# A decoder layer on one core: weight sums ordered behind a plain block, and three PSUM bank assignments changed

## The chip, the core and the metric

The kernel runs on one core of a Trainium2 chip. The metric is the device time of one execution in microseconds (us), and the time of a kernel is the median of several executions. The profile beside it was taken of one further execution.

## What is computed

The reference is one layer over 512 tokens of 1024 features, all in float32: a half-step gated feed-forward block (FFN), a token mixer, and a second half-step FFN. In the mixer half of the width runs a gated linear recurrence and the other half attention with eight heads, both from one input projection.

```python
x = x + 0.5 * swiglu(rms_norm(x, ffn1_norm), w_gate, w_up, w_down)   # 1024 -> 2816 -> 1024
h = rms_norm(x, mix_norm)
xr, gate, q, k, v = split(h @ w_in)              # five parts of 512 features
y_rnn = rg_lru(conv4(xr)) * gelu(gate)
y_att = stick_breaking(rms_norm(q), rms_norm(k), v)   # 8 heads of 64
x = x + concat(rms_norm(y_rnn), rms_norm(y_att)) @ w_out
x = x + 0.5 * swiglu(rms_norm(x, ffn2_norm), ...)
```

## The kernel before

Activations lie transposed, features on the 128 partitions and the 512 tokens along the row, so `x` is eight tiles of 128x512. For accuracy every float32 operand is split into a rounded high part and the remainder (names with `h` and `l`: `h_ga` and `l_ga` for a gate weight, `xh` and `xl` for an activation, `hha` and `hla` for a hidden block), and a product is three matmuls, high by high, low by high, high by low (`mm3`). ScalarE (ACT) makes the high parts and VectorE (DVE) the low ones. Names end in `a` for the first FFN and `b` for the second.

**An FFN** has 22 blocks of 128 hidden features, each with a gate product `pg` and an up product `pu`. The first six are *plain* (three pairs of two): `products` runs 24 matmuls of 128x512 each for `pg` and `pu`, and `plain` then multiplies both by the norm factor `rb` into `gg` and `uu` (L267, L269), applies Silu to `gg` (L268), multiplies the two (L270) and splits the result (L254, L255). The other sixteen are computed in pairs by a seven-product scheme (`fast`). It needs sums of the activations (`bs`, split into `xh_s` and `xl_s`, made by `operands`), and, for every pair and each of gate and up, four sums of quarters of the weights: `matrix` loads the pair's weights into `raw` (tiles `rg`, `ru`) and VectorE makes the sums into `sums` (tiles `sg`, `su`) by the four additions L326, L328, L329 and L330. The second overwrites a quarter that the first has read, so the other three follow the first. Down-projections `pd` follow after blocks 6, 12, 18 and 22, eight products each, and VectorE adds them to `x` (L433).

**The mixer** projects the eight normed tiles `xh_m`, `xl_m` by `project(j)` (for j from 0 to 3: two products `pxr` and `pga`, alternating over the eight tiles for j = 0) and by `project_qkv` (for q, k and v four token blocks each, `pq`, `pk`, `pv`, the weights arriving in four parts `kk`). `norm_heads` makes normed tiles `natq` and `natk` from `pq` and `pk`: ScalarE squares, VectorE sums (`m8`, L688 and L689), GpSimd (POOL) takes the power (`r8`, L691), VectorE multiplies (`nat`, L694). `turn` transposes each `nat` on TensorE into `ptq` or `ptk` (L710). Behind the v products `rnn_out` prepares the recurrence's output (`yrh`, `yrl`, L644 and L646), and the first products with `w_out` (weights `h_o`, `l_o`) follow.

**PSUM.** `psum` opens a pool of the eight banks for a stage and `bank(name, tag)` takes one. FFN: four banks tagged `b` and four `y`; mixer: six `b` and two `y`. A bank that is taken again waits for the last reader of what lay in it, also across stages. In a stage of the mixer `y` holds the norm's two small products (`pst_m`, `psr_m`), the gates `pa`, `px`, and the turned k.

**Order.** A scheduler of the language sets each engine's order when the kernel is built, by its own estimate of times; engines then run strictly in that order and wait on semaphores. `tc.issue_after(ins)` puts what is traced inside it behind `ins` on the same engine. `tc.high_priority` raises a load and its split. All loads stand on SyncE's one queue (SP), which issues them in order as weight buffers come free.

Of the kernel before, what the change touches and what calls it, by code (L numbers as in the profile page):

```python
# [23 lines left out]
NB = T // P  # L24
# [4 lines left out]
PLAIN = 6  # L29
# [19 lines left out]
def hybrid_layer_kernel(  # L49
# [17 lines left out]
    nc = tc.nc  # L67
# [18 lines left out]
    def f32(ap):  # L86
        return ap.bitcast(F32)

    def bank(name, tag="b"):
        return banks["pool"].tile([P, T], F32, tag=tag, name=name, bufs=banks["tags"][tag])  # L90
# [40 lines left out]
    def weights_early(*args):  # L131
        with tc.high_priority(offset=200):
            return weights(*args)
# [80 lines left out]
    def ffn(name, xn, wg, wu, wd, first, done):  # L214
        def products(f, between=None):
            n = f"{name}{f}"
            c = f % 2 * KD * P
            gh, gl = weights(wg[f // 2][:, c : c + KD * P], f"g{n}")
            uh, ul = weights(wu[f // 2][:, c : c + KD * P], f"u{n}")
            pg, pu = (bank(f"{p}{n}", "y" if between else "b") for p in ("pg", "pu"))  # L220
            each = ((pg, gh, gl), (pu, uh, ul))
            order = [(e, k) for e in each for k in range(KD)]
            if f == 0:
                order = [(e, k) for k in range(KD) for e in each]
            for i, ((pt, wh, wl), k) in enumerate(order):
                s = slice(k * P, (k + 1) * P)
                mm3(pt, wh[:, s], wl[:, s], xn.h[k], xn.l[k], k == 0, k == KD - 1)
                if between and i == KD - 1:
                    between()
            return pg, pu  # L230
# [5 lines left out]
        with tc.tile_pool(name=f"ffn_{name}", bufs=1, reuse_waits="tile") as fp:  # L236

            def flat(ap):
                return ap.rearrange("p c t -> p (c t)")

            def pair_tiles(p):
                n = f"{name}{p}"
                g = fp.tile([P, 4, TH], F32, tag="g", name=f"gg{n}", bufs=2)
                u = fp.tile([P, 4, TH], F32, tag="u", name=f"uu{n}")
                return g, u
# [12 lines left out]
            def plain(p, i):  # L258

                g, u = pair_tiles(p)  # L260
                for t in range(2):
                    f = 2 * p + t
                    if f == len(ahead):
                        ahead.append(products(f))
                    gg, uu = flat(g[:, 2 * t : 2 * t + 2, :]), flat(u[:, 2 * t : 2 * t + 2, :])
                    pg, pu = ahead[f]
                    nc.vector.tensor_mul(gg, pg, rb)  # L267
                    nc.scalar.activation(gg, gg, AF.Silu)  # L268
                    nc.vector.tensor_mul(uu, pu, rb)  # L269
                    nc.vector.tensor_mul(uu, uu, gg)  # L270
                return split(u, p, i)


# [44 lines left out]

            def matrix(w, c, p):

                n = f"{c}{name}{p}"
                q = 4 * P
                raw = fp.tile([P, 4, q], F32, tag="raw", name=f"r{n}", bufs=3)
                nc.sync.dma_start(raw, w[p].rearrange("p (s w) -> p s w", s=4))
                sums = fp.tile([P, 3, q], F32, tag="sums", name=f"s{n}", bufs=2)
                nc.vector.tensor_add(sums[:, 1, :], raw[:, 2, :], raw[:, 0, :])  # L326
                s1 = raw[:, 0, :]
                nc.vector.tensor_add(s1, s1, raw[:, 1, :])  # L328
                nc.vector.tensor_add(sums[:, 0, :], raw[:, 2, :], s1)  # L329
                nc.vector.tensor_add(sums[:, 2, :], raw[:, 3, :], sums[:, 0, :])  # L330
                groups = [
                    [raw[:, 2:4, :]],
                    [sums[:, 0:1, :], raw[:, 0:1, :]],
                    [sums[:, 1:3, :]],
                    [raw[:, 1:2, :]],
                ]
                ws = []

                def get(group):
                    if group < len(ws):  # L340
                        return ws[group]
                    width = sum(a.shape[1] for a in groups[group]) * q
                    hi = wpool.tile([P, width], F32R, tag="wh", name=f"h_{n}{group}", bufs=4)
                    lo = wpool.tile([P, width], F32R, tag="wl", name=f"l_{n}{group}", bufs=4)
                    o = 0
                    for a in groups[group]:
                        a = flat(a)
                        to = slice(o, o + a.shape[1])
                        nc.scalar.copy(hi[:, to], a)
                        nc.vector.tensor_sub(lo[:, to], a, f32(hi[:, to]))  # L350
                        o += a.shape[1]
                    ws.append((hi, lo))
                    return hi, lo

                px, py = (bank(f"p{i}{n}", "b")[:, :TH] for i in "xy")

                def product(pt, group, half, b, start):
                    wh, wl = get(group)
                    for k in range(KD // 2):
                        s = slice((half * 4 + k) * P, (half * 4 + k + 1) * P)  # L360
                        bh, bl = held[k, b]
                        for i, (l, r) in enumerate(((wh, bh), (wh, bl), (wl, bh))):
                            nc.tensor.matmul(  # L363
                                pt, l[:, s], r, start=start and k == 0 and i == 0,
                                stop=k == KD // 2 - 1 and i == 2, skip_group_check=True,
                            )

                return [
                    (px, 0, 0, B11, True), (py, 0, 1, B21, True),
                    (px, 1, 0, T2, False), (py, 1, 1, T1, True),  # L370
                    (px, 2, 0, T3, False), (py, 2, 1, B22, False),
                    (px, 3, 0, T4, False),
                ], product
# [39 lines left out]
            for nf in CHUNKS:  # L413
                hs = []
                for i in range(nf // 2):
                    p = f0 // 2 + i
                    hs += (plain if 2 * p < PLAIN else fast)(p, i)
                last = f0 + nf == NF
                for k in range(KD):
                    n = f"{name}{f0}_{k}"  # L420
# [6 lines left out]
                    for t0, t1 in zip(cuts, cuts[1:]):  # L427
                        t = slice(t0, t1)
                        pt = bank(f"pd{n}_{t0}", "y")
# [17 lines left out]
    pt = bank("warm")  # L447
# [110 lines left out]
    def project(j, between=None):  # L558

        ws = [weights_early(w_rg[c], f"{n}{j}") for c, n in ((j, "xr"), (NJ + j, "ga"))]  # L560
        pts = [bank(f"p{n}{j}") for n in ("xr", "ga")]
        order = [(i, k) for i in range(2) for k in range(KD)]
        if j == 0:
            order = [(i, k) for k in range(KD) for i in range(2)]
        for i, k in order:
            s = slice(k * P, (k + 1) * P)
            (wh, wl), ks = ws[i], [kk for ii, kk in order if ii == i]
            mm3(pts[i], wh[:, s], wl[:, s], nm.h[k], nm.l[k], k == ks[0], k == ks[-1])
            if between and (i, k) == order[KD - 1]:
                between()  # L570
        return pts
# [86 lines left out]
    v = []  # L658

    def project_qkv(c, n, between):  # L660
        pts = [bank(f"p{n}{b}") for b in range(NB)]
        done = 0
        for kk in range(KD // 2):
            wh, wl = weights_early(w_qkv[c, kk], f"{n}{kk}")
            ks = (2 * kk, 2 * kk + 1)
            order = [(k, b) for k in ks for b in range(NB)]
            if kk == KD // 2 - 1 or n == "v" and kk == 0:
                order = [(k, b) for b in range(NB) for k in ks]
            for k, b in order:
                t = slice(b * P, (b + 1) * P)  # L670
                s = slice((k % 2) * DR, (k % 2 + 1) * DR)
                mm3(pts[b], nm.h[k][:, t], nm.l[k][:, t], wh[:, s], wl[:, s], k == 0, k == KD - 1)
                done += 1
                if done in between:
                    between[done]()
        return pts
# [27 lines left out]

    def turn(n, nats):
        for b, nat in enumerate(nats):
            pt = bank(f"pt{n}{b}", "b" if n == "q" else "y")
            for j in range(NJ):
                s = slice(j * P, (j + 1) * P)
                nc.tensor.transpose(pt[:, s], nat[:, s], ident)  # L710
            gain = gq if n == "q" else gk
            dh = qkT[n + "h"][:, :, b * P : (b + 1) * P]
            dl = qkT[n + "l"][:, :, b * P : (b + 1) * P]
            src = pt.rearrange("p (j t) -> p j t", j=NJ)
            nc.scalar.activation(dh, src, AF.Copy, scale=gain)
            nc.vector.scalar_tensor_tensor(
                dl, src, gain, f32(dh), op0=ALU.mult, op1=ALU.subtract
            )
# [288 lines left out]
```

## Time and profile before

| | |
|---|---|
| time, three executions | 934.52, 935.11, 940.92 us; median 935.11 us |
| the profiled execution, its own time | 937.35 us |
| its span, from first to last instruction | 935.6 us |
| its mean granted TensorE clock | 0.995 of full speed |
| TensorE busy | 916.2 us of the span |
| VectorE, ScalarE, GpSimd busy | 677.0, 443.3, 109.6 us |
| DMA | 89.51 MB, mean 96 GB/s |

A row of the timeline gives the start, the duration, the engine, the source line, the operation with its output and inputs, and in square brackets how long the engine had been idle and what ended that. A row of the waits gives the waiting and the releasing operation, the total in us, how often, and the longest. A row of the windows gives a stretch, its length, then for each engine the busy time and the number of instructions, then the granted TensorE clock (1.00 is full speed), the DMA share and GB/s. Matmuls overlap: a 128x512 one lasts 0.39 us in the rows and starts every 0.23 us.

### The profile page before, as it was taken

The numbers are of one execution on the slowest core, as the hardware profiler recorded it, in microseconds if no ns is written. First come the engines' busy times: TensorE is split into PE (matmuls) and PEld (weight loads), VectorE is DVE, ScalarE is ACT, GpSimd is POOL, SyncE is SP. The second block draws the span as 40 slices with busy tenths as digits, with TensorE's granted clock in tenths as the row PEclk, the third lists the DMA queues.
The fourth block names the chain that finished last, engine by engine and source line by source line (L and its number), as shares of the span: only waits on it lengthen the run. The fifth ranks groups of instructions, "written<-read, shape, count | busy, mean of one in ns | idle before, by whom it ended". The sixth has DMA issues, their size and how long they took to land.

```text
span 935.6 us, 13626 instructions
## 1 busy us (share of the span) xinstructions
PE 916.2 (98%) x5410; PEld 800.3 (86%) x5410; DVE 677.0 (72%) x1007; ACT 443.3 (47%) x739; POOL 109.6 (12%) x79
## 2 busy tenths in 40 slices
PE   8899999999999998999989999999999999999998
PEld 6788899889988997888866667888899989998997
DVE  7699588648864859756669867778768846884673
ACT  7154355425542546345656744454345524552451
POOL 4000000000000005554351121400000000000000
PEclk9999999999999999999999999999999999999999
DMA  7621222522252123222110112532222422243102
GB/s 248 241 75 51 68 91 91 162 64 91 91 168 74 47 90 112 91 91 90 46 56 35 47 67 87 204 104 68 85 90 91 141 85 91 91 143 100 46 24 90
DMA packets 26943, 89.51 MB, mean 96 GB/s; under 512 B 2944, under 2 KB 5248, under 8 KB 22784
## 3 DMA queue, kind: packets, MB, share of 16 engines
q1 hardware_dynamic: 26880, 88.65, 28.1%
q8 instruction: 42, 0.69, 0.3%
q14 instruction: 21, 0.17, 0.1%
HBM read 86.54 MB, written 2.10 MB: 95 GB/s over the span
## 4 chain that ended last, share of the span: by engine, by line
PE 87%; DVE 6%; DMA 2%; issue 2%; ACT 1%; POOL 1%; SPq 0%; DVEq 0%; ACTq 0%; POOLq 0%
PE pxgb L363 5%; PE pxga L363 5%; PE pxub L363 5%; PE pxua L363 5%; PE pdb L136 4%; PE pdb L137 4%; PE pdb L138 4%; PE pda L136 4%; PE pda L138 4%; PE pda L137 4%; PE pyga L363 4%; PE pygb L363 4%; PE pyua L363 4%; PE pyub L363 4%; PE pga L136 1%
## 5 line engine op out<-in xcount | busy, mean ns | idle before, releaser
L137 PE MATMUL pdb<-hlb,h_db 128*128 128x512 f32 (+1 forms) x180 | 68.9, 385 | 0.0
L138 PE MATMUL pdb<-hhb,l_db 128*128 128x512 f32 (+1 forms) x180 | 68.7, 385 | 0.0
L137 PE MATMUL pda<-hla,h_da 128*128 128x512 f32 x176 | 68.2, 389 | 0.0
L138 PE MATMUL pda<-hha,l_da 128*128 128x512 f32 x176 | 68.0, 389 | 0.0
L136 PE MATMUL pdb<-hhb,h_db 128*128 128x512 f32 (+1 forms) x180 | 67.3, 385 | 0.0
L136 PE MATMUL pda<-hha,h_da 128*128 128x512 f32 x176 | 66.7, 389 | 0.0
L433 DVE SCALAR_TENSOR_TENSOR x<-pdb,x 128x512 f32<-128x512 f32 (+1 forms) x33 | 21.9, 673 | 51.1 <-PE pdb L138 51.1
L433 DVE SCALAR_TENSOR_TENSOR x<-pda,x 128x512 f32<-128x512 f32 x32 | 21.7, 687 | 43.6 <-PE pda L138 43.6
L166 POOL TENSOR_TENSOR sqa_m<-sqa_m,sq_m 128x512 f32<-128x512 f32 x7 | 11.7, 1675 | 322.8 <-issue 318.8
L126 ACT CAST h_db<-r_db 128x768 fp32r<-128x768 f32 (+1 forms) x28 | 24.2, 868 | 40.2 <-PE pdb L137 20.0
L126 ACT CAST h_da<-r_da 128x768 fp32r<-128x768 f32 (+1 forms) x28 | 24.2, 868 | 37.0 <-PE pda L137 20.0
L136 PEld LDWEIGHTS pdb<-hhb,h_db 128*128 128x128 f32 x180 | 33.9, 188 | 6.5
L138 PEld LDWEIGHTS pdb<-hhb,l_db 128*128 128x128 f32 x180 | 33.8, 188 | 6.6
L137 PEld LDWEIGHTS pdb<-hlb,h_db 128*128 128x128 f32 x180 | 33.8, 188 | 6.5
L137 PEld LDWEIGHTS pda<-hla,h_da 128*128 128x128 f32 x176 | 33.1, 188 | 6.7
L138 PEld LDWEIGHTS pda<-hha,l_da 128*128 128x128 f32 x176 | 33.1, 188 | 6.7
L136 PEld LDWEIGHTS pda<-hha,h_da 128*128 128x128 f32 x176 | 33.1, 188 | 6.6
L363 PE MATMUL pxga<-xl_sa,h_ga 128*128 128x256 f32 x128 | 36.2, 283 | 0.0
L363 PE MATMUL pxga<-xh_sa,l_ga 128*128 128x256 f32 x128 | 36.2, 283 | 0.0
L363 PE MATMUL pxgb<-xh_sb,l_gb 128*128 128x256 f32 x128 | 36.2, 283 | 0.0
L363 PE MATMUL pxgb<-xl_sb,h_gb 128*128 128x256 f32 x128 | 36.2, 283 | 0.0
L363 PE MATMUL pxub<-xh_sb,l_ub 128*128 128x256 f32 x128 | 36.2, 283 | 0.0
(397 smaller groups left out, 3157.1 us busy)
## 6 DMA issues: line engine op xcount, KB each, us to landing
r_da<-in_wd SPq DMA_DIRECT2D x24, 384.0 KB, 3.2
r_db<-in_wd SPq DMA_DIRECT2D x24, 384.0 KB, 3.2
rga<-in_wg SPq DMA_DIRECT2D x8, 1024.0 KB, 4.8
rua<-in_wu SPq DMA_DIRECT2D x8, 1024.0 KB, 4.8
rgb<-in_wg SPq DMA_DIRECT2D x8, 1024.0 KB, 4.9
rub<-in_wu SPq DMA_DIRECT2D x8, 1024.0 KB, 4.7
r_gb<-in_wg SPq DMA_DIRECT2D x6, 512.0 KB, 3.6
r_ub<-in_wu SPq DMA_DIRECT2D x6, 512.0 KB, 3.5
```

Of the source, the lines that this page charges most:

```text
L126: nc.scalar.copy(hi, raw)
L136: nc.tensor.matmul(out_, wh, ah, start=start, stop=False)
L137: nc.tensor.matmul(out_, wh, al, start=False, stop=False)
L138: nc.tensor.matmul(out_, wl, ah, start=False, stop=stop)
L166: nc.gpsimd.tensor_add(self.acc, self.acc, sq)
L363: nc.tensor.matmul(pt, l[:, s], r, start=start and k == 0 and i == 0, stop=k == KD // 2 - 1 and i == 2, skip_group_check=True,)
L433: nc.vector.scalar_tensor_tensor(x[k][:, t], pt[:, t], 0.5, x[k][:, t], op0=ALU.mult, op1=ALU.add)
```

## The change

Three things change. In `plain`, the VectorE instruction of L270 of blocks 0 to 3 is kept, and the first of the four weight sums of every pair is put behind the last one kept, that of block 3. In `project(0)`, the second product `pga` takes a bank of tag `y` instead of `b`. In `project_qkv`, the third and fourth token block of v take `y`, and `turn` takes `b` for k as well as for q.

```diff
                     nc.vector.tensor_mul(uu, pu, rb)
-                    nc.vector.tensor_mul(uu, uu, gg)
+                    last = nc.vector.tensor_mul(uu, uu, gg)
+                    if f < PLAIN - 2:
+                        plain.last = last
...
-                nc.vector.tensor_add(sums[:, 1, :], raw[:, 2, :], raw[:, 0, :])
+                with tc.issue_after(plain.last.ins):
+                    nc.vector.tensor_add(sums[:, 1, :], raw[:, 2, :], raw[:, 0, :])
...
-        pts = [bank(f"p{n}{j}") for n in ("xr", "ga")]
+        pts = [bank(f"p{n}{j}", "y" if (j, n) == (0, "ga") else "b") for n in ("xr", "ga")]
...
-        pts = [bank(f"p{n}{b}") for b in range(NB)]
+        pts = [bank(f"p{n}{b}", "y" if n == "v" and b > 1 else "b") for b in range(NB)]
...
-            pt = bank(f"pt{n}{b}", "b" if n == "q" else "y")
+            pt = bank(f"pt{n}{b}")
```

No instruction is added or taken away, and no load moves on SyncE's queue. The new lines shift the source lines behind them by two to five. In the built program the banks are, by number: `pga` of `project(0)` lay in bank 5, in which the last of the first FFN's down-projection products (the one for `x` tile 7) had lain, and now lies in bank 6, that of `x` tile 5; the third and fourth v products lay in the banks of the second and third `pk` and now lie in banks 7 and 6, which the last gates leave; the four `ptk` lay in banks 6 and 7 by turns and now each lies in the bank of its own `pk`.

**VectorE at the head of the first FFN**, from the norm's `m_a` on (`first_p`, `pga` and `pua` are products of the plain blocks). Before:

```order
L181 TENSOR_SCALAR m_a<-pst_a 128x4
L326 TENSOR_TENSOR sga_958<-rga_956 128x512
L328 TENSOR_TENSOR rga_956<-rga_956 128x512
L329 TENSOR_TENSOR sga_958<-rga_956 128x512
L330 TENSOR_TENSOR sga_958<-rga_956,sga_958 128x512
L128 TENSOR_TENSOR l_ga_520<-r_ga_516,h_ga_518 128x1024
L326 TENSOR_TENSOR sua_967<-rua_965 128x512
L267 TENSOR_TENSOR gga_420<-first_p_118,rb_a 128x512
```

Now, the head and, some 25 rows on, the place to which the sums went:

```order
L181 TENSOR_SCALAR m_a<-pst_a 128x4
L128 TENSOR_TENSOR l_ga_520<-r_ga_516,h_ga_518 128x1024
L267 TENSOR_TENSOR gga_420<-first_p_118,rb_a 128x512
...
L128 TENSOR_TENSOR l_ua_592<-r_ua_588,h_ua_590 128x1024
L270 TENSOR_TENSOR uua_437<-uua_437,gga_436 128x512
L330 TENSOR_TENSOR sga_958<-rga_956 128x512
L330 TENSOR_TENSOR sua_967<-rua_965 128x512
L255 TENSOR_TENSOR hla_509<-uua_437,hha_508 128x512
```

The eight sums of the first pair stood ahead of and among the first plain blocks' multiplications and stand now behind block 3, spread between the work on blocks 3 to 5. The second FFN has the same move.

**VectorE behind the k products.** Before:

```order
L694 SCALAR_TENSOR_TENSOR natk0_4346<-pk0_4180,r_m_3666,r8k0_4344 128x512
L688 TENSOR_REDUCE m8k2_4359<-nsqk2_4357 128x8
L689 TENSOR_SCALAR m8k2_4359<-m8k2_4359 128x8
L694 SCALAR_TENSOR_TENSOR natk1_4355<-pk1_4181,r_m_3666,r8k1_4353 128x512
L688 TENSOR_REDUCE m8k3_4368<-nsqk3_4366 128x8
L689 TENSOR_SCALAR m8k3_4368<-m8k3_4368 128x8
L694 SCALAR_TENSOR_TENSOR natk2_4364<-pk2_4182,r_m_3666,r8k2_4362 128x512
L694 SCALAR_TENSOR_TENSOR natk3_4373<-pk3_4183,r_m_3666,r8k3_4371 128x512
L646 SCALAR_TENSOR_TENSOR yrl0_4429<-gel0_3752,vec_71,yrh0_4427 128x512
```

Now, from behind `natk0` and the sum `m8k2` on:

```order
L650 SCALAR_TENSOR_TENSOR yrl0_4429<-gel0_3752,vec_71,yrh0_4427 128x512
L650 SCALAR_TENSOR_TENSOR yrl1_4435<-gel1_3772,vec_71,yrh1_4433 128x512
L128 TENSOR_TENSOR l_o0_0_4590<-r_o0_0_4586,h_o0_0_4588 128x512
L694 TENSOR_SCALAR m8k2_4359<-m8k2_4359 128x8
L699 SCALAR_TENSOR_TENSOR natk1_4355<-pk1_4181,r_m_3666,r8k1_4353 128x512
L693 TENSOR_REDUCE m8k3_4368<-nsqk3_4366 128x8
L650 SCALAR_TENSOR_TENSOR yrl2_4442<-gel2_4040,vec_71,yrh2_4440 128x512
L694 TENSOR_SCALAR m8k3_4368<-m8k3_4368 128x8
L699 SCALAR_TENSOR_TENSOR natk2_4364<-pk2_4182,r_m_3666,r8k2_4362 128x512
L650 SCALAR_TENSOR_TENSOR yrl3_4449<-gel3_4163,vec_71,yrh3_4447 128x512
L128 TENSOR_TENSOR l_o0_1_4750<-r_o0_1_4746,h_o0_1_4748 128x512
L699 SCALAR_TENSOR_TENSOR natk3_4373<-pk3_4183,r_m_3666,r8k3_4371 128x512
```

The four `yrl` and two of the `l_o`, which stood behind all four `natk`, now stand between them.

**TensorE in the v products.** Before, the 96 matmuls ran `pv0` and `pv1` ahead (46 matmuls), then `pv2` and `pv3`; two of the turned k stood before the last 14 matmuls and two behind them. Now all four blocks take each part of the weights in turn, and the turned k stand together ahead of the last 15 matmuls:

```order
L138 MATMUL pv1_4376<-h_v3_4498,xl_m6_3519 128x512
L715 MATMUL ptk0_4511<-ident_77,natk0_4346 128x128 x4
L715 MATMUL ptk1_4518<-ident_77,natk1_4355 128x128 x4
L715 MATMUL ptk2_4525<-ident_77,natk2_4364 128x128 x4
L715 MATMUL ptk3_4532<-ident_77,natk3_4373 128x128 x4
L136 MATMUL pv1_4376<-h_v3_4498,xh_m7_3538 128x512
```

TensorE reaches `natk3` with 81 of the 96 v matmuls behind it, where before all 96 were.

## The prediction

> **What bounds the kernel now.** I read the page's summary first, then the chain that ended last, then TensorE's waits, and then went to each wait in the timeline.
>
> ```profile
> span 935.6 us, 13626 instructions
> PE 916.2 (98%) x5410; PEld 800.3 (86%) x5410; DVE 677.0 (72%) x1007; ACT 443.3 (47%) x739; POOL 109.6 (12%) x79
> PE 87%; DVE 6%; DMA 2%; issue 2%; ACT 1%; POOL 1%; SPq 0%; DVEq 0%; ACTq 0%; POOLq 0%
> ```
>
> TensorE is busy for 916.2 of 935.6 us, and the chain that ended last runs on it for 87%. The change takes no matmul away, so it can gain only where TensorE stands still or is slowed. TensorE's waits, with total, count and longest:
>
> ```profile
> PE pw L828 <- DVE be L820: 3.3, 3, 1.5
> PE pga L136 <- DVE gga L267: 2.9, 1, 2.9
> PE pga L136 <- DVE x L433: 2.9, 1, 2.9
> PE pv L136 <- DVE natk L694: 2.5, 1, 2.5
> ```
>
> The first lies in the attention, where nothing moves. The other three are the places of the three edits, and together they are 8.3 us: this is what is to be had from waits, and the rest of the working is on how much of each comes back, and whether a new wait takes its place.
>
> **Weight sums behind block 3, first FFN.** Where the second wait ends, and what VectorE did ahead of it:
>
> ```profile
> 36.96 1.05 ACT L126 CAST h_ga<-r_ga 128x1024 fp32r<-128x1024 f32 x1 [5.49 <-PE pga L137]
> 40.70 0.69 DVE L326 TENSOR_TENSOR sga<-rga 128x512 f32<-128x512 f32 x1 [6.69 <-DMA rga<-in_wg]
> 43.49 1.22 DVE L128 TENSOR_TENSOR l_ga<-r_ga,h_ga 128x1024 fp32r<-128x1024 f32 x1
> 44.62 0.68 DVE L326 TENSOR_TENSOR sua<-rua 128x512 f32<-128x512 f32 x1
> 45.23 0.68 DVE L267 TENSOR_TENSOR gga<-first_p,rb_a 128x512 f32<-128x512 f32 x1
> 45.97 0.50 PE L136 MATMUL pga<-xh_a,h_ga 128*128 128x512 f32 x1 [2.91 <-DVE gga L267]
> ```
>
> VectorE sat idle for 6.69 us until the weights of the first pair of the seven-product blocks arrived, then made four of their sums, `l_ga`, a fifth sum, and only then `gga`, whose end frees a PSUM bank. With the sums gone, the head of VectorE's queue is `l_ga`, whose input `h_ga` ends at 36.96 + 1.05 = 38.01. `l_ga` then ends near 39.2 and `gga` near 39.9. TensorE reached the wait at 45.97 − 2.91 = 43.06, so the bank is free 3 us early: **−2.9**. For this to hold, nothing behind may be late in its place. The sums have to be done somewhere, 8 × 0.60 (44.62 to 45.23, from one row's start to the next when the engine is full), 4.8 us, between the work on blocks 3 to 5; VectorE starts this stretch over 5 us earlier than it did. Between this place and the mixer no other wait of TensorE of 2 us stands in the list, so an earlier TensorE arrives earlier at the mixer's wait as well.
>
> **The clock behind that wait.** The granted clock in two stretches just behind a wait of this length (the other's row stands below):
>
> ```profile
> 46.00:50.00 4.00, 4.00 (x11) 3.17 (x12) 4.00 (x7) 3.15 (x5) 0.00 (x0) 0.57 0.28 110
> 366.00:376.00 10.00, 10.00 (x50) 8.36 (x48) 8.70 (x31) 4.59 (x8) 1.70 (x1) 1.00 0.42 159
> ```
>
> ```profile
> 53.13 0.39 PE L136 MATMUL pua<-xh_a,h_ua 128*128 128x512 f32 x1
> 58.57 0.39 PE L136 MATMUL pga<-xh_a,h_ga 128*128 128x512 f32 x1
> ```
>
> Behind the wait of 2.91 us the clock is 0.57, and the 24 matmuls of this `pga` take 53.13 − 45.97 = 7.16 us; the next 24 take 58.57 − 53.13 = 5.44. So 1.7 us are lost to the clock. Behind the mixer's wait, as long as this one, the clock is 1.00. One such wait in two cost the clock in this execution; whether it did in the three that were timed isn't shown. I take half in the median: **−0.85**, bounds 0 and −1.7.
>
> [...]
>
> **Bank of the mixer's second product.** The third wait:
>
> ```profile
> 359.75 0.68 DVE L433 SCALAR_TENSOR_TENSOR x<-pda,x 128x512 f32<-128x512 f32 x1
> 361.80 0.39 PE L138 MATMUL pxr<-xh_m,l_xr 128*128 128x512 f32 x1
> 364.26 0.68 DVE L433 SCALAR_TENSOR_TENSOR x<-pda,x 128x512 f32<-128x512 f32 x1
> 365.09 0.47 PE L136 MATMUL pga<-xh_m,h_ga 128*128 128x512 f32 x1 [2.90 <-DVE x L433]
> 370.08 0.74 DVE L152 SCALAR_TENSOR_TENSOR xl_m<-x,vec,xh_m 128x512 fp32r<-128x512 f32 x1
> 375.38 0.94 PE L173 MATMUL pst_m<-ones,sqa_m 128*128 128x1 f32 x8
> ```
>
> `pga` took the bank of the last `x` tile, which VectorE left at 364.26 + 0.68. The new bank is that of tile 5, left at 359.75 + 0.68 = 360.43, ahead of the last `pxr` matmul at 361.80. `pga` then starts at 362.03, one step of 0.23 behind it: **−2.9** by the idle of the row (365.09 − 362.03 less that step). What is late next is the last `xl_m`, which VectorE ends at 370.82 whatever TensorE does. The products with tile 7 are the last 6 of 48 and need `xl_m` as their last operand: 48 matmuls run from 361 to 375.38, without the wait to 372.4, so tile 7's turn comes at about 371.1 and its `xl_m` matmul later still. The cover is 0.3 us or a little more; if it is gone, each 0.1 us of lateness costs 0.1.
>
> **The v blocks and the turned k.** The fourth wait and the chain that follows it:
>
> ```profile
> 460.42 0.39 PE L136 MATMUL pv<-h_v,xh_m 128*128 128x512 f32 x1
> 473.84 0.50 PE L136 MATMUL pv<-h_v,xh_m 128*128 128x512 f32 x1 [2.45 <-DVE natk L694]
> 477.06 3.25 POOL L691 TENSOR_TENSOR r8k<-m8k,mhalf 128x8 f32<-128x8 f32 x2
> 478.74 0.75 DVE L694 SCALAR_TENSOR_TENSOR natk<-pk,r_m,r8k 128x512 f32<-128x512 f32 x1 [1.31 <-POOL r8k L691]
> 480.34 0.75 DVE L694 SCALAR_TENSOR_TENSOR natk<-pk,r_m,r8k 128x512 f32<-128x512 f32 x1 [0.85 <-POOL r8k L691]
> 481.01 1.41 DVE L646 SCALAR_TENSOR_TENSOR yrl<-gel,vec,yrh 128x512 fp32r<-128x512 f32 x2
> 482.33 0.68 DVE L128 TENSOR_TENSOR l_o<-r_o,h_o 128x512 fp32r<-128x512 f32 x1
> 482.18 1.04 PE L710 MATMUL ptk<-ident,natk 128*128 128x128 f32 x8
> 487.41 0.95 PE L173 MATMUL pst_r<-ones,sqa_r 128*128 128x1 f32 x8
> ```
>
> The third `pv` waited until `natk` had read the bank it takes. The v blocks now have banks that the gates left long before, so 81 of the 96 v matmuls run from 460.42 without a stop, at 0.23 us each, to 478.8 (81 × 0.227). Then the four turned k stand in a row, some 0.4 us each, by the row at 482.18 that holds two of them in 1.04 us, the last step's tail with it. Three end by 480.0; the fourth needs `natk3`. That one hangs on POOL's `r8k`, which ends at 477.06 + 3.25 = 480.31, and POOL's order is as it was. But VectorE now has `yrl3` and an `l_o` between `natk2` (478.74) and `natk3`: 0.66 + 0.66 + 0.60 puts `natk3` at about 480.7, its end at 481.4. So TensorE **waits anew for some 1.5 us**, at the turned k; behind it stand only the turn, 0.4, and 15 matmuls, 3.4: `pst_r` at about 485.4 instead of 487.41, a gain of 2.0. If VectorE's moved rows run slower beside POOL, it is less. A row of the second FFN beside POOL's sums shows it:
>
> ```profile
> 590.00 10.91 POOL L166 TENSOR_TENSOR sqa_b<-sqa_b,sq_b 128x512 f32<-128x512 f32 x7 [21.77 <-issue]
> 594.90 1.46 DVE L326 TENSOR_TENSOR sgb<-rgb 128x512 f32<-128x512 f32 x1 [4.36 <-DMA rgb<-in_wg]
> ```
>
> The same sum that took 0.69 at 40.70 took 1.46 here. One `l_o` slowed by that makes `natk3` 0.7 later, a gain of 1.3. I take **−1.6**; the bounds are 0 (the new wait as long as the old) and −2.45.
>
> The Trainium skill (*GPSIMD Engine Reference*, "1. Specifications") says that GpSimd shares its SBUF interfaces with VectorE and that VectorE instructions with two SBUF inputs contend with it. This speaks against putting `yrl` and `l_o` between POOL's steps; 1.46 against 0.69 agrees. By that rule the edit is worth 1.3, without it 2.0.
>
> **The same sums in the second FFN.** No wait of TensorE is listed there, so there is none to remove; the question is what the moved sums disturb.
>
> ```profile
> 629.68 0.69 DVE L269 TENSOR_TENSOR uub<-pub,rb_b 128x512 f32<-128x512 f32 x1 [0.63 <-PE pub L138]
> 640.56 0.69 DVE L269 TENSOR_TENSOR uub<-pub,rb_b 128x512 f32<-128x512 f32 x1 [0.90 <-PE pub L138]
> 643.50 0.69 DVE L255 TENSOR_TENSOR hlb<-uub,hhb 128x512 fp32r<-128x512 f32 x1 [0.35 <-ACT hhb L254]
> 646.00 0.69 DVE L267 TENSOR_TENSOR ggb<-pgb,rb_b 128x512 f32<-128x512 f32 x1 [1.81 <-PE pgb L138]
> 655.99 0.69 DVE L255 TENSOR_TENSOR hlb<-uub,hhb 128x512 fp32r<-128x512 f32 x1
> 661.67 0.39 PE L138 MATMUL pdb<-hhb,l_db 128*128 128x512 f32 x1
> ```
>
> 4.8 us of sums go into a stretch in which VectorE idles 0.63 + 0.90 + 0.35 + 1.81 = 3.7, so it comes out 1.1 late. The last `hlb` ends at 656.7 and the down-projection needs it near 661.5: 4.8 of slack. **0**, and up to 4.8 − 3.7 = 1.1 more lateness would still be covered.
>
> **The sum**, against the profiled execution's 937.35 (its span and 1.75 around it): −2.9 − 2.9 − 1.6 = −7.4 gives 929.95, with all of the clock's 1.7 928.25. The median of the runs, 935.11, lies 2.24 below that execution, and what made the difference isn't shown. From the median: 935.11 − 7.4 − 0.85 = **926.9**.
>
> **Rivals.** *All of it goes:* the `natk` chain keeps up, and the v products' whole 2.45 is gained with the step behind it, some 2.9, and the clock's 1.7 besides: 2.9 + 2.9 + 2.9 + 1.7 = 10.4, 924.7. For it: POOL's `r8k` ends at 480.31, at TensorE's arrival; against it, the two rows now ahead of `natk3`.
>
> *The turned k's wait takes the place of the one removed:* the `l_o` waits for ScalarE's weight half or POOL slows it, `natk3` comes 1.6 later, and the third edit brings 0: 935.11 − 5.8 − 0.85 = 928.5, and 930.2 if the longer idle costs the clock 1.7. For it: the four turns stand together now, where before two had matmuls behind them to fill.
>
> *The second edit doesn't do what it says:* bank 6 is held by another reader, or `xl_m` is as late as the bank was. 926.9 + 2.9 = 929.8. Against it: the row at 359.75.
>
> *Slower:* the sums land on the path. In both FFNs they stand ahead of the rows that make the last plain halves; it decides from 4.8 us of lateness, when the first down-projection waits. If VectorE's rows ran at the 1.46 of 594.90 rather than 0.69, eight sums would cost 6 more, and with both FFNs waiting for all of their 4.8, 9.6 are lost: 926.9 + 9.6 = 936.5, and 938.2 with the clock. For it: the slack is finite and this part of VectorE is nearly full. Against it: POOL's work in the second FFN ends at 601, long before.
>
> **How the numbers follow.** Forecast 0.63, all of it goes 0.17, the turned k 0.10, the bank 0.05, slower 0.05. A measurement of this kernel tells about 1% from no change, 9.35 us, so faster by that begins below 925.76. The forecast's own spread (the clock's 0.85 either way, the v products from 1.3 to 2.0) reaches 925.6 to 928.1. The range takes in the first three rivals and half a microsecond beyond the lowest: 924.2 to 930.4. All of the case in which everything goes and a seventh of the forecast lie below 925.76: 0.17 + 0.09 = 0.26; beyond +1%, 0.02, a part of the last rival with further stalls behind it; the rest, 0.72, within.
>
> **What would show it.** Right: no wait of `pga` for `gga` or for `x`; a granted clock of 1.00 where 0.57 stood; `pga` of the mixer 0.23 behind the last first `pxr`; no wait of `pv` for `natk`, but one of 1 to 2 us of `ptk` for `natk`; no wait of `pda` or `pdb` for `hla` or `hlb`. The prediction is wrong if a wait of over 2 us stands at `ptk`, if the first down-projection waits in either FFN, if the 0.57 appears behind another wait, or if the three waits go and the time doesn't follow them.

## The result, and the profile after

| | before | changed |
|---|---|---|
| median of six executions | 935.87 us | 927.61 us |
| lowest to highest | 934.52 to 940.92 | 926.88 to 929.08 |
| profiled execution, its own time | 937.35 | 926.92 |

The ratio of the times is 0.9907, with a 95% interval of 0.9883 to 0.9931: 8.3 us faster in the median. The forecast was 926.9, and 927.61 was measured. The interval excludes no change; the 0.9% is less than the 1% that the prediction took for what can be told from none, and its chances gave 0.72 to a change of that size.

The changed kernel's page, with the span, the busy times and the chain that ended last:

```profile
span 925.1 us, 13631 instructions
PE 912.2 (99%) x5410; PEld 798.5 (86%) x5410; DVE 674.1 (73%) x1007; ACT 442.5 (48%) x739; POOL 111.8 (12%) x79
PE 89%; DVE 6%; issue 2%; ACT 1%; DMA 1%; POOL 1%; SPq 1%; DVEq 0%; ACTq 0%; POOLq 0%
```

The five instructions more than before are on none of these engines, whose counts are the same. Its waits of TensorE:

```profile
PE pw L833 <- DVE be L825: 3.3, 3, 1.5
PE ptk L715 <- DVE natk L699: 1.8, 2, 1.3
PE pst_t L173 <- POOL sqa_t L166: 1.1, 1, 1.1
```

The three waits named in the prediction are gone, and one has come, at the turned k. To see where the time went, one takes rows that both kernels have and subtracts their starts, stretch by stretch. Of the kernel before, TensorE's timeline has these beside those of the prediction:

```profile
361.34 0.39 PE L136 MATMUL pxr<-xh_m,h_xr 128*128 128x512 f32 x1
606.30 0.95 PE L173 MATMUL pst_b<-ones,sqa_b 128*128 128x1 f32 x8
651.24 0.39 PE L136 MATMUL pdb<-hhb,h_db 128*128 128x512 f32 x1
```

And of the changed kernel:

```profile
42.97 0.39 PE L136 MATMUL pga<-xh_a,h_ga 128*128 128x512 f32 x1
...
356.62 0.39 PE L136 MATMUL pxr<-xh_m,h_xr 128*128 128x512 f32 x1
...
357.07 0.39 PE L138 MATMUL pxr<-xh_m,l_xr 128*128 128x512 f32 x1
357.30 0.39 PE L136 MATMUL pga<-xh_m,h_ga 128*128 128x512 f32 x1
...
367.54 0.95 PE L173 MATMUL pst_m<-ones,sqa_m 128*128 128x1 f32 x8
...
452.56 0.39 PE L136 MATMUL pv<-h_v,xh_m 128*128 128x512 f32 x1
...
470.93 1.03 PE L715 MATMUL ptk<-ident,natk 128*128 128x128 f32 x8
472.46 0.63 PE L715 MATMUL ptk<-ident,natk 128*128 128x128 f32 x4 [0.50 <-DVE natk L699]
474.38 0.63 PE L715 MATMUL ptk<-ident,natk 128*128 128x128 f32 x4 [1.30 <-DVE natk L699]
...
478.28 0.94 PE L173 MATMUL pst_r<-ones,sqa_r 128*128 128x1 f32 x8
...
595.88 0.95 PE L173 MATMUL pst_b<-ones,sqa_b 128*128 128x1 f32 x8
...
640.82 0.39 PE L136 MATMUL pdb<-hhb,h_db 128*128 128x512 f32 x1
```

| stretch | before | changed | difference |
|---|---|---|---|
| start to the mixer's first `pxr` | 361.34 | 356.62 | −4.72 |
| from there to `pst_m` | 14.04 | 10.92 | −3.12 |
| `pst_m` to the first `pv` | 85.04 | 85.02 | −0.02 |
| first `pv` to `pst_r` | 26.99 | 25.72 | −1.27 |
| second FFN, `pst_b` to the first `pdb` | 44.94 | 44.94 | 0 |

The first line holds two things. `pga` of the first FFN starts at 42.97 instead of 45.97, which is 3.0; the other 1.7 is the clock, as the stretch behind it shows (the columns are those of the windows of before):

```profile
46.00:50.00 4.00, 4.00 (x20) 3.30 (x19) 4.00 (x8) 1.70 (x4) 0.00 (x0) 1.00 0.34 98
```

Twenty matmuls where there had been eleven, at a clock of 1.00 instead of 0.57. The first four differences come to 9.13. The last 1.3 of the profiled execution's 10.43 lie between the first `po` behind `pst_r` and `pst_b`, a stretch that no edit touches: 118.08 before (488.22 to 606.30) and 116.79 now (479.09 to 595.88). It holds two clock drops before, at 500 and 534, and one now, at 554, behind a wait of 1.1 (another stands at the very end, at 924):

```profile
553.84 1.05 PE L173 MATMUL pst_t<-ones,sqa_t 128*128 128x1 f32 x8 [1.14 <-POOL sqa_t L166]
```

```profile
555.00:559.00 4.00, 4.00 (x12) 3.08 (x12) 0.09 (x1) 0.00 (x0) 1.02 (x1) 0.57 0.38 131
```

In all profiles of this document the stretch takes 116.76 to 116.79 with one drop (four profiles) and 117.70 to 118.11 with two (nine), and four of these nine are of kernels with all three edits. So the runs don't put this 1.3 down to the change.

### The profile page after: what moved, and what is told of

The parts are those of the page before. It is cut to its first block, busy times and chain, and to the rows that moved or that the text cites. A ratio compares the mean times of both kernels' runs of the same rounds, so it can differ in the third digit from the quotient of the medians.

```text
span 925.1 us, 13631 instructions
## 1 busy us (share of the span) xinstructions
PE 912.2 (99%) x5410; PEld 798.5 (86%) x5410; DVE 674.1 (73%) x1007; ACT 442.5 (48%) x739; POOL 111.8 (12%) x79
## 4 chain that ended last, share of the span: by engine, by line
PE 89%; DVE 6%; issue 2%; ACT 1%; DMA 1%; POOL 1%; SPq 1%; DVEq 0%; ACTq 0%; POOLq 0%
PE pxgb L367 5%; PE pxga L367 5%; PE pxub L367 5%; PE pxua L367 5%; PE pdb L136 4%; PE pdb L138 4%; PE pdb L137 4%; PE pda L138 4%; PE pda L137 4%; PE pda L136 4%; PE pygb L367 4%; PE pyga L367 4%; PE pyua L367 4%; PE pyub L367 4%; PE pga L136 2%
## 5 line engine op out<-in xcount | busy, mean ns | idle before, releaser
L367 PE MATMUL pxua<-xh_sa,l_ua 128*128 128x256 f32 x128 | 36.2, 283 | 0.0
```

What stands on the lines that cost most here:

```text
L367: nc.tensor.matmul(pt, l[:, s], r, start=start and k == 0 and i == 0, stop=k == KD // 2 - 1 and i == 2, skip_group_check=True,)
```

## Experiments

Ten kernels ran beside these two, one of them twice. The ratios are to runs of the kernel before on the same chip; since its own times spread over several microseconds, most verdicts rest on stretches of the trace.

**One edit at a time.** The sums alone:

```diff
-                    nc.vector.tensor_mul(uu, uu, gg)
+                    last = nc.vector.tensor_mul(uu, uu, gg)
+                    if f < PLAIN - 2:
+                        plain.last = last
...
-                nc.vector.tensor_add(sums[:, 1, :], raw[:, 2, :], raw[:, 0, :])
+                with tc.issue_after(plain.last.ins):
+                    nc.vector.tensor_add(sums[:, 1, :], raw[:, 2, :], raw[:, 0, :])
```

> The kernel before with the sums of the first pair behind block 3's last product in both FFNs, and no bank changed. Theory (the three edits add up, each worth the wait that it removes): no wait of pga for gga, the wait of the mixer's pga for x stays at 2.9 and that of pv for natk at 2.5; the mixer's first product starts 2.9 us earlier in the trace, 4.7 if the granted clock behind the removed wait was below 1 before; time 2.9 to 4.7 below the kernel before. Rival (a later wait swallows the gain): the mixer's wait grows by what TensorE arrives earlier, and the time is that of before within 1 us.

Median 934.12, ratio 0.9968 (0.9953 to 0.9983). Its waits, and the stretch behind the mixer's:

```profile
PE pga L136 <- DVE x L436: 2.9, 1, 2.9
PE pv L136 <- DVE natk L697: 2.4, 1, 2.4
```

```profile
360.00:364.00 4.00, 3.74 (x10) 2.96 (x11) 4.00 (x8) 3.98 (x7) 2.07 (x2) 0.57 0.01 3
```

The wait for `gga` is gone and `pxr` starts at 356.51, 4.83 earlier. No later wait grew, so the rival falls. But the wait for `x`, at whose end the clock had been 1.00 before, now has 0.57 behind it, and `pxr` to `pst_m` takes 1.6 longer than before. The clock's part is not bound to one place.

The bank alone:

```diff
-        pts = [bank(f"p{n}{j}") for n in ("xr", "ga")]
+        pts = [bank(f"p{n}{j}", "y" if (j, n) == (0, "ga") else "b") for n in ("xr", "ga")]
```

> The kernel before with only the bank of the mixer's first pga changed; every engine's order is that of before. Theory: the wait of pga for x goes, the stretch from the first pxr to pst_m shortens by 2.9 us, the wait of 2.9 at the first FFN's gga and that of 2.5 at pv stay; time 2.9 below the kernel before. Rival (the last xl_m takes its place): a wait of pxr or pga for xl_m or xh_m of some 2 us, and the time within 1 us of before.

Median 932.84, ratio 0.9962 (0.9944 to 0.9979).

```profile
PE pv L136 <- DVE natk L694: 2.5, 1, 2.5
PE pga L136 <- DVE gga L267: 2.4, 1, 2.4
```

```profile
359.31 0.39 PE L136 MATMUL pxr<-xh_m,h_xr 128*128 128x512 f32 x1
...
370.22 0.95 PE L173 MATMUL pst_m<-ones,sqa_m 128*128 128x1 f32 x8
```

No wait for `x` and none for `xl_m`; the stretch takes 10.91 instead of 14.04, 3.13 less. The rival falls.

The banks of v and of the turned k alone:

```diff
-        pts = [bank(f"p{n}{b}") for b in range(NB)]
+        pts = [bank(f"p{n}{b}", "y" if n == "v" and b > 1 else "b") for b in range(NB)]
...
-            pt = bank(f"pt{n}{b}", "b" if n == "q" else "y")
+            pt = bank(f"pt{n}{b}")
```

> The kernel before with only the banks of two v blocks and of the turned k changed. Theory: no wait of pv for natk, waits of ptk for natk of 1.8 in all, pst_r 1.3 us earlier, counted from the first pv matmul; time 1.3 below the kernel before, plus or minus what the granted clock does in the attention behind it. Rival (the gain is the clock's alone, or the new wait is as long as the old): pst_r moves by less than 0.5.

Median 936.52, ratio 0.9994 (0.9979 to 1.0008): no difference that the times can tell, with 1.3 us less still inside the interval. TensorE's rows, and the stretch behind the second wait:

```profile
460.61 0.39 PE L136 MATMUL pv<-h_v,xh_m 128*128 128x512 f32 x1
...
480.53 0.63 PE L710 MATMUL ptk<-ident,natk 128*128 128x128 f32 x4 [0.52 <-DVE natk L694]
482.45 0.76 PE L710 MATMUL ptk<-ident,natk 128*128 128x128 f32 x4 [1.29 <-DVE natk L694]
...
487.94 0.95 PE L173 MATMUL pst_r<-ones,sqa_r 128*128 128x1 f32 x8
```

```profile
482.00:486.00 4.00, 3.55 (x12) 2.90 (x13) 3.54 (x6) 1.38 (x2) 0.00 (x0) 0.60 0.40 131
```

The new waits are there as expected. First `pv` to `pst_r` is 27.33, 0.34 more than before, though it holds less waiting: behind the turned k the clock is 0.60 over 4 us, which costs 4 × 0.40 = 1.6, and without that it would be some 1.3 shorter. So the stretch did not come out as expected in this execution: by its sign, `pst_r` moving by less than 0.5, the rival came. But the new wait is shorter than the old, 1.8 against 2.5, and the clock behind it accounts for the rest. In the changed kernel, where no drop stands there, the same stretch takes 25.72.

The sums in the second FFN alone (the edit of the sums, with this line instead; in the first FFN they stay):

```diff
-                with tc.issue_after(plain.last.ins):
+                with tc.issue_after(plain.last.ins) if name == "b" else nullcontext():
```

> The kernel before with the sums of the first pair behind block 3's last product in the second FFN alone. Theory: no wait was there and none comes, TensorE's rows from 600 us on keep their distances within 0.2 us, time within 1 us of before. Rival (the sums land on VectorE's way to the first down-projection): a wait of pdb for hlb of 1 to 4.8 us, time later by as much.

Median 935.85, ratio 0.9997 (0.9983 to 1.0011). No wait of `pdb`; `pst_b` to `pdb` takes 44.94, as in every kernel here. The rival falls.

**How far the sums are from mattering.** The first sum made three or seven times more often (`n`), for gate and up:

```diff
                 with tc.issue_after(plain.last.ins):
                     nc.vector.tensor_add(sums[:, 1, :], raw[:, 2, :], raw[:, 0, :])
+                    if p == PLAIN // 2 and c[0] in 'gu':
+                        for _ in range(n):
+                            nc.vector.tensor_add(sums[:, 1, :], raw[:, 2, :], raw[:, 0, :])
```

> The changed kernel with the first of the four sums made three times more for gate and up of the first pair, in both FFNs: 6 more rows of 0.60 us on VectorE behind block 3, 3.6 us in each FFN; the output is the same. Theory (4.5 to 4.8 us of slack ahead of the first down-projection): no wait of pda or pdb for hla or hlb, time that of the changed kernel within 1 us. Rival (the sums lie on the path): 3.6 us in each FFN, 7 us slower.

> As the run with three more, but with seven: 14 rows, 8.4 us in each FFN. Theory: the last hla comes at 81.3 + 8.4 - 0.6 = 89.1 and is needed at 85.8, so a wait of pda for hla of about 3.3 us, the same in the second FFN, and 6.6 us slower than the changed kernel, up to 10 if the clock drops behind both. Rival (the sums lie on the path from the first): 8.4 in each, 17 us slower; other rival (VectorE catches up elsewhere): no wait.

Medians 928.20 and 927.87, ratios 0.9896 (0.9876 to 0.9915) and 0.9898 (0.9877 to 0.9919). No matmul of `pda` or `pdb` waits in either. With 8.4 us more in each FFN, the stretch from the first down-projection to the first `px` grew by 0.3 in each, in the second from 32.64 to 32.91. There a weight load, not a matmul, waits, and not for `hlb` but for the low part of a down-projection weight; the first FFN has the same wait:

```profile
641.21 0.39 PE L136 MATMUL pdb<-hhb,h_db 128*128 128x512 f32 x1
...
674.12 0.28 PE L370 MATMUL pxgb<-xh_sb,h_gb 128*128 128x256 f32 x1
```

```profile
658.58 0.19 PEld L138 LDWEIGHTS pdb<-hhb,l_db 128*128 128x128 f32 x1 [0.39 <-DVE l_db L128]
```

With three more the theory held; with seven it failed, and the third possibility, that VectorE catches up elsewhere, came but for this 0.3. It is not a clean test of the slack, though: the scheduler had put other rows, such as the later sums, behind the last `hla`, which starts 8.1 us behind the first `pda` instead of 5.0, 3.1 later and not 8.4. What it shows is that work of this size on VectorE finds nearly all its room there, and that `l_da` and `l_db` are late first.

**The new wait.** The four `yrl` put behind `natk3`, on the changed kernel:

```diff
-            nc.vector.scalar_tensor_tensor(
-                l, gel[j], v1(C_RN + j), f32(h), op0=ALU.mult, op1=ALU.subtract
-            )
+            with tc.issue_after(box["nat"].ins):
+                nc.vector.scalar_tensor_tensor(
+                    l, gel[j], v1(C_RN + j), f32(h), op0=ALU.mult, op1=ALU.subtract
+                )
...
-            nc.vector.scalar_tensor_tensor(
+            box["nat"] = nc.vector.scalar_tensor_tensor(
                 heads(nat),
```

> The changed kernel with the four yrl put behind natk3 on VectorE; the first two l_o stay where they are. Theory (the new wait at the turned k is due to VectorE's moved rows, which hold up m8k and so POOL's r8k as well as natk): natk3 ends 0.9 us earlier, counted from natk0, the waits of ptk for natk fall from 1.8 to about 0.8, pst_r comes 1.0 earlier. Rival (POOL's own chain sets it): natk3 and the waits stay within 0.3 us.

Median 927.01, ratio 0.9887 (0.9865 to 0.9908), beside the changed kernel's 0.9907 not to be told apart. VectorE and POOL in the changed kernel:

```profile
465.19 0.75 DVE L699 SCALAR_TENSOR_TENSOR natk<-pk,r_m,r8k 128x512 f32<-128x512 f32 x1 [2.86 <-POOL r8k L696]
...
466.45 1.41 DVE L650 SCALAR_TENSOR_TENSOR yrl<-gel,vec,yrh 128x512 fp32r<-128x512 f32 x2
467.78 0.68 DVE L128 TENSOR_TENSOR l_o<-r_o,h_o 128x512 fp32r<-128x512 f32 x1
468.38 1.29 DVE L694 TENSOR_SCALAR m8k<-m8k 128x8 f32<-128x8 f32 x1
469.58 0.74 DVE L699 SCALAR_TENSOR_TENSOR natk<-pk,r_m,r8k 128x512 f32<-128x512 f32 x1
...
473.49 0.74 DVE L699 SCALAR_TENSOR_TENSOR natk<-pk,r_m,r8k 128x512 f32<-128x512 f32 x1
```

```profile
467.99 1.65 POOL L166 TENSOR_TENSOR sqa_r<-sqa_r,sq_r 128x512 f32<-128x512 f32 x1
469.75 1.65 POOL L696 TENSOR_TENSOR r8k<-m8k,mhalf 128x8 f32<-128x8 f32 x1
471.80 1.64 POOL L696 TENSOR_TENSOR r8k<-m8k,mhalf 128x8 f32<-128x8 f32 x1 [0.40 <-DVE m8k L694]
```

And VectorE in the experiment:

```profile
465.17 0.75 DVE L700 SCALAR_TENSOR_TENSOR natk<-pk,r_m,r8k 128x512 f32<-128x512 f32 x1 [2.87 <-POOL r8k L697]
...
467.03 0.17 DVE L695 TENSOR_SCALAR m8k<-m8k 128x8 f32<-128x8 f32 x1
468.04 0.75 DVE L700 SCALAR_TENSOR_TENSOR natk<-pk,r_m,r8k 128x512 f32<-128x512 f32 x1 [0.84 <-POOL r8k L697]
...
472.51 0.75 DVE L700 SCALAR_TENSOR_TENSOR natk<-pk,r_m,r8k 128x512 f32<-128x512 f32 x1 [0.26 <-POOL r8k L697]
```

`natk3` follows `natk0` by 7.34 instead of 8.30, 0.96 earlier, and `pst_r` the first `pv` by 24.79 instead of 25.72. The theory holds: the moved rows held up `m8k`, and through it POOL. TensorE's one wait left there, 1.0, is ended by ScalarE by the profile, and half of the gain is given back a few rows on, where `po` starts only 0.5 earlier.

All four turned k behind the last v matmul, on the changed kernel:

```diff
-    pv = project_qkv(2, "v", {12: rnn_out, 27: lambda: turn("k", nk)})
+    pv = project_qkv(2, "v", {12: rnn_out, 32: lambda: turn("k", nk)})
```

> The changed kernel with the four turned k behind the last v matmul on TensorE. Theory (natk3 is late by 1.8 for a place that stands 15 matmuls early): no wait of ptk for natk, pst_r 1.8 us earlier counted from the first pv (23.9 instead of 25.7), nothing late behind it; time 1.8 below the changed kernel. Rival (kTl then comes too late for the attention): a wait of pz for kTl or kTh of 1 to 2 us and no gain.

Median 928.22, ratio 0.9898 (0.9879 to 0.9918). No wait of `ptk`, and `pst_r` 23.51 behind the first `pv`, 2.2 less; but then

```profile
478.83 0.50 PE L136 MATMUL po<-yrh,h_o 128*128 128x512 f32 x1 [1.46 <-DVE kTl L721]
```

The wait went on to `po`, which VectorE's `kTl`, the last reader of a turned k, holds up. At `po` 0.6 of the 2.2 are left. The rival was right in kind, though not at `pz`.

The turned k spread instead, two at the old place, the third behind six more matmuls of v and the fourth behind another six:

```diff
-    def turn(n, nats):
-        for b, nat in enumerate(nats):
+    def turn(n, nats, blocks=range(NB)):
+        for b in blocks:
+            nat = nats[b]
...
-    pv = project_qkv(2, "v", {12: rnn_out, 27: lambda: turn("k", nk)})
+    pv = project_qkv(2, "v", {12: rnn_out, 27: lambda: turn("k", nk, (0, 1)), 29: lambda: turn("k", nk, (2,)), 31: lambda: turn("k", nk, (3,))})
```

> The changed kernel with the turned k spread on TensorE: two where all four stood, the third behind two more products of v, the fourth behind another two. Theory (the new wait is one of place on TensorE alone, and the banks that the turned k hold become free soon enough when only the last one comes later): no wait of ptk over 0.3, pst_r 1.8 us earlier counted from the first pv (23.9 instead of 25.7), po without a wait; time 1.8 below the changed kernel. Rival (as when all four came last, the banks held until kTl pass the wait on to po): po waits over 1 us and the gain at po is 0.6.

Median 925.79, ratio 0.9875 (0.9851 to 0.9899).

```profile
473.10 0.60 PE L716 MATMUL ptk<-ident,natk 128*128 128x128 f32 x4
474.92 0.60 PE L716 MATMUL ptk<-ident,natk 128*128 128x128 f32 x4
476.06 0.95 PE L173 MATMUL pst_r<-ones,sqa_r 128*128 128x1 f32 x8
476.87 0.48 PE L136 MATMUL po<-yrh,h_o 128*128 128x512 f32 x1
```

No wait is left: the first `pv` is at 452.48, so `pst_r` follows by 23.58 and `po` by 24.39 instead of 26.53, 2.1 less. It has the lowest median of all; against the changed kernel the intervals of the ratios overlap, so that is shown by the trace and only suggested by the times.

**The clock.** The kernel before, with its first two waits filled by matmuls that nobody reads (lines left out keep the last matmul of a product in `mm3.last` and put the waiting product behind the fill):

```diff
+    def fill(name, w, a, count):
+        pt = bank(name, "y")
+        last = mm3.last
+        for _ in range(count):
+            with tc.issue_after(last.ins):
+                last = nc.tensor.matmul(pt, w, a, start=True, stop=True)
+        return last
...
+            filled = fill(f"f{n}", gh[:, 0:P], xn.h[0], 9) if (name, f) == ("a", 3) else None
...
+            filled = fill("fm", ws[0][0][:, s], nm.h[0], 12) if (j, i, k) == (0, 1, 0) else None
```

> The kernel before with both its waits kept, but TensorE kept at work in them: 9 matmuls whose result nobody reads ahead of the first FFN's pga that waits for gga, and 12 ahead of the mixer's pga that waits for x. Theory (the drop of the granted clock comes from TensorE's idling, not from what stands there): no clock under 0.95 in the 6 us behind either place; the waits together cost what they did, and the time is 0 to 2 below the kernel before. Rival (the drop comes with the place or the load): a drop behind one place or both, as in 4 of the 8 such waits profiled so far.

> The same kernel once more for another profile: theory, again no clock under 0.95 behind either place; rival, a drop in every second.

Median of the first 935.49, ratio 0.9976 (0.9960 to 0.9993); the second, one execution, 936.43. The ratio is 2.2 us of gain. In the profile `pga` starts at 45.45 instead of 45.97, but without the fill that start lay anywhere from 44.66 to 45.97, so the runs don't show that the fill moved it. The stretches behind both places, of the first kernel:

```profile
45.00:49.00 4.00, 4.00 (x19) 3.00 (x18) 4.00 (x8) 2.73 (x4) 0.00 (x0) 1.00 0.34 131
363.00:367.00 4.00, 3.99 (x18) 3.29 (x19) 4.00 (x7) 3.97 (x8) 2.07 (x2) 1.00 0.04 10
```

Both are at 1.00 in the second as well. That one has 0.63 from 471 to 475, behind the wait of `pv` for `natk`, which was not filled. Counted over all profiles here, waits of 1.7 to 2.9 for `gga` and `x` had a drop behind them in 4 cases of 8 when TensorE stood idle, and in none of 4 when it was at work. These few cases alone could be chance. The timed executions point the same way: the mean granted clock was 0.995 to 0.998 in all twelve of the filled kernel, and under 0.995 in nine of the seventeen of the kernel before beside them. That idling at these places brings the drop is thus supported. Length alone does not decide: the wait of `pv` for `natk`, 2.4 to 2.5, had a drop behind it in one of the six profiles that have it, and in the changed kernel one stood behind a wait of 1.1. What decides between a wait that does and one that does not was not tried.

## Why the prediction was right

**Sums, first FFN (−2.9).** Measured 3.0 in the trace, and alone 4.83 with the clock. Nothing behind was late, and with 8.4 us more in the place to which the sums went only 0.3 was.

**The clock (half of 1.7).** In the profiled execution all of it came back. That either may be the case is borne out: the drop stands behind some waits and not behind others of the same length, and in the run with the sums alone, where the first wait is gone, it stands behind the next. One sign that the prediction named against itself, the 0.57 behind another wait, did come, at `pst_t` in the changed kernel's profile; the profile has one drop within its work all the same, where that of before has three. The 0.85 for the median was a mean over cases and has no measurement of its own, but the mean granted clock of the timed executions bears on it. Over 63 executions of the kernel before, on the three chips of the experiments, it was 0.989 to 0.996, median 0.995, and their mean time rose from 935.0 us at 0.996 to 940.7 at 0.989. The changed kernel's six have 0.996 to 0.998, median 0.996. A thousandth of the span is 0.9 us, so the medians differ by about what was forecast, as far as figures rounded to a thousandth can tell. The Trainium skill (*TensorE: Matmul & The Clock Gate*, "Part 1: The HAM clock gate (the "warmup" mystery)") has the slower clock after at least one idle window of some 3.4 us. The traces here don't agree: the drops followed waits of 2.9 and less.

**Bank (−2.9).** Measured 3.12 and 3.13. The prediction's own starts, 365.09 and 362.03, already give 3.06: no step of 0.23 had to be taken off, since the matmul behind the wait starts one step behind the last `pxr` (357.07, 357.30). No wait for `xl_m` came, and the cover was as narrow as the 0.3 forecast: the last `xl_m` ended at 366.12, and the first matmul that reads it started at 366.37.

**v and the turned k (−1.6, from 1.3 to 2.0).** Measured 1.27, at the lower end. The wait that takes the old one's place was foreseen at 1.5 and is 1.8, 0.5 of it already for `natk2`, and `natk3` ended 21.67 behind the first `pv` instead of the 20.98 forecast (481.4 less 460.42), 0.7 late. The step that was off is this: "POOL's order is as it was", from which the end of `r8k` was taken over unchanged. The order was the same, but not the times. `yrl` and `l_o` stand ahead not only of `natk3` but of `m8k2`'s second step, which then took 1.29 instead of 0.17 beside POOL's addition and held up `natk1`, `m8k3` and POOL's last `r8k`, which waited 0.40. With `yrl` out of the way 0.96 came back. The prediction looked at the row that TensorE waits for and not at the chain that feeds it. The 1.3 that the prediction worked out for a slowed `l_o` is the right size by luck: `yrl` and `l_o` kept 0.7 and 0.68, and the row that was stretched is the small `m8k`. The Trainium skill (*GPSIMD Engine Reference*, "1. Specifications") names VectorE instructions with two SBUF inputs among those that contend with GpSimd. This place does not bear that out: the `l_o` at 467.78, which has two inputs, kept its 0.68 beside POOL's addition from 467.99 on, and the `m8k` behind it, which has one tensor as input, did not; whether it ran in the two-port mode that the page names as well, no run here shows.

**Second FFN (0).** Right: 44.94 in both. The last `hlb` of this place starts 5.02 behind the first `pdb` instead of 4.75 (645.84 and 655.99), so it came 0.3 late and not the 1.1 forecast. The prediction's last figure there is wrong: a slack of 4.8 with 1.1 of it used leaves 3.7, not 1.1.

**Rivals.** That everything goes fell by the wait at the turned k; that this wait eats the whole edit is wrong by size (1.27 are left), though in the profile of that edit alone the clock dropped behind the wait and nothing was gained. The bank was free. The slower case is far: even 14 rows added in each FFN cost 0.3 in each.

**The sum.** Three waits bring 3.0 + 3.1 + 1.3 = 7.4, which is the prediction's firm part, with two terms off by 0.1 and 0.2 up and one by 0.3 down; that they cancel is luck. The median's 8.3 leaves 0.9 for the clock, but the interval of the ratio reaches 2.2 us to either side, so the times alone don't show this term.

## What to carry to other kernels

A wait of TensorE is worth its idle time and, in some executions, the slower clock behind it; a change that swaps a wait for a shorter one keeps that second risk. When rows are moved on one engine, the row to check is not only the one that somebody waits for but each earlier row that feeds another engine's chain toward it. A wait that comes from an early place in a queue was best mended here by moving only the late items back a little: all four turned k at the end passed most of the wait on, and two of them moved back by six and twelve matmuls removed it.

## What the runs showed of the hardware

The length of the first wait was not a property of the program: with VectorE's order at the head unchanged it was 2.9, 2.4 and 2.8 in three profiles (before, and the two with only banks changed) and 1.7 in that with only the second FFN's sums moved, and the first sum, which waits for a transfer (`rga`), started at 40.70, 40.26, 39.52 and 39.40.

The VectorE row `m8k` of 128x8 takes 0.17 us beside GpSimd's power of the same size (474.41 in the kernel before). Beside POOL's 128x512 addition it took 1.29, ending at 469.67, with the addition ending at 469.64; the addition took 1.65 instead of 1.29. Each seems to have held the other up; the runs don't show by what.
